# Expert lookup on one core: a quarter of the gathered down rows through TensorE, part of the coefficient products through ScalarE

## The chip, the cores and the metric

The kernel runs on one core of a Trainium2 chip. TensorE (PE) does matrix products, VectorE (DVE) and ScalarE (ACT) element-wise work and reductions, GpSimd (POOL) and SyncE (SP) issue transfers; 16 DMA engines of the core carry them. TensorE's clock has two levels, 2.4 and 1.2 GHz; the profile prints the granted one as 1.00 and 0.50. The metric is the time of one execution on the device, in microseconds (us), of the median run.

## What is computed

Two transformer blocks over 256 tokens of width 2048, in float32. Only the expert lookup of the first block ("PEER") is touched. Each token makes 8 queries (heads); each head picks 16 of 16,384 experts. An expert is one row of `expert_down` and one of `expert_up`; the token's activation is the dot product with the first, its output a weighted sum of the second:

```python
def peer(x, w_query, sub_keys, expert_down, expert_up):
    qry = (xt @ w_query).reshape(T, H, 2, PEER_HALF_DIM)
    s = jnp.einsum('thpd,phnd->thpn', qry, sub_keys).astype(jnp.float32)
    top_s, top_i = lax.top_k(s, K)
    ...
    best_s, best_pos = lax.top_k(cand_s.reshape(T, H, K * K), K)
    expert_idx = jnp.take_along_axis(cand_i.reshape(T, H, K * K), best_pos, axis=-1)
    gates = jax.nn.softmax(best_s, axis=-1).astype(x.dtype)
    ...
        u = expert_down[ib]
        act = jax.nn.gelu(jnp.einsum('td,thkd->thk', xb, u), approximate=False)
        vv = expert_up[ib]
        return jnp.einsum('thk,thkd->td', gb * act, vv)
```

## The kernel before

A tile is 128 tokens, one per partition; there are two, t = 0 and 1. With 8 heads each this makes 16 steps that are called heads 0 to 15 here. The lookup runs in these parts, all of them in one function.

**Queries.** `w_peer_query` is multiplied in four column blocks c (L681 on). SP loads the weights, ScalarE casts them to a high part (L253), VectorE makes the low part (L254, tile wlo), TensorE adds three products (L293 to L295, tile pq). ScalarE copies the result to qT (L685); TensorE and ScalarE make the scores of tile 0 block by block (`scores`, L677, L679), those of tile 1 when the first route of tile 1 is recorded. hn (L687) holds the normed tokens, one per partition.

**Routes.** `route(t, hd)` finds the 16 experts of a head on VectorE, 26 instructions or so from L569 to L606; L599 writes the expert indices (eidx) that the gathers need, L604 is an Exp on ScalarE.

**Down rows.** `peer_down(t, hd)`: for each of 16 experts k, POOL issues an indirect DMA that gathers one row of 2048 numbers per token (L612, 128 x 2048, 1.05 MB); two gathers share a row tile. VectorE multiplies the row with hn and sums along it (L621, CUSTOM_DVE_ANT_0 in the profile), one number per token, into dots. After 16 rows ScalarE applies Gelu (L625) and VectorE the gate (L626, output pk, since coef lies in that tile): this is a head's end.

**Coefficients of tile 0**, in the background of heads 8 to 11 (`store_coefs`, `coef_chunk`): for four tokens at a time ScalarE makes one-hot rows of the first index half (Square L648, Relu L649, tile ab), VectorE one-hot rows of the second half scaled by the coefficient (L667), TensorE multiplies them (L669, pcc), ScalarE copies the result to a chunk (L670). 32 such steps make 4 chunks of 2 MB; three go to DRAM (ct_d, ACT's queue), the last stays. Then `onehots_ahead` makes one-hot rows of tile 1 (tile oh) on ScalarE until the stage ends. Behind head 15 tile 1's products follow (L669 again), up to 1615 us, and then the "up" stage streams `expert_up`.

**What sets the order.** A scheduler places each instruction on its engine from the order of recording; `route_to` records routes some heads ahead, and the generator `bg` is advanced once for each pair of rows. Memory comes from pools: seven "big" tiles of 16 KB per partition (h, hn, hhi and hlo, qT, mhi and mlo earlier, row tiles, chunks), three raw tiles, two e8 tiles, and in PSUM two of 1024 columns (`acc`) and four of 512 (`pst`). A tile that is not free makes its writer wait, and POOL's gathers are issued in order, so a gather that waits holds up all later ones. Before the projection's end at 898 two row tiles are free, then five, while chunks are held three to five, then four.

```python
row = bigt([P, 2, D], name="row")
for i in range(2):
    gather(row[:, i, :], dn_d, eidx[:, t, hd, k + i:k + i + 1])
for i in range(2):
    V.tensor_tensor_reduce(out=row[:, i, :], in0=row[:, i, :], in1=hn[:, t, :], ...)
yield
```

## Time and profile before

| | us |
|---|---|
| median of 3 runs | 3214.01 (3211.68 to 3218.35) |
| the profiled execution | 3219.45, its span 3217.7 |
| the stage that is touched, from the first gather to head 15's end | 827 to 1574 |
| VectorE busy in the whole span | 2535.2 (79%) |
| TensorE busy in the whole span | 2555.4 (79%), mean granted clock 0.892 |
| DMA, mean over the span | 279 GB/s |

The page cuts the span into 40 slices. Slices 11 to 20 are the stage: VectorE and DMA stand at 9 tenths there, TensorE at 0 to 4 with its clock near 5 tenths. Elsewhere TensorE is at 9 and VectorE below. A view by stretch adds busy times of each engine between two moments; views by line group equal instructions; a timeline lists them in order of start, with the idle time before each and what ended it. An instruction's duration can overlap the next one's, so the distance of two starts is given as its pace.

### The profile page before, as it was taken

Reading aid. Unit: us, or ns where it says so; the run is one execution under the profiler, and the core shown is the slowest. Engines: PE = TensorE matmul, PEld = TensorE weight load, DVE = VectorE, ACT = ScalarE, POOL = GpSimd, SP = SyncE. Lnnn points to the kernel's source line nnn. Section 1 sums busy time; section 2 is a strip of 40 time slices with the busy share of each in tenths; the row PEclk is TensorE's granted clock in tenths of the full one; section 3 lists DMA queues with packets and bytes.
Section 4 is the critical chain, followed back from the end, with each engine's and each line's share of the span. In section 5 each row is a group of like instructions: output and inputs, shape, how many; then the busy total and the mean of one; then the engine's idle time right before and its main releaser. Section 6 shows DMA issues by size and latency. Waiting matters only on the chain. (4 is left out here: it accounts for less than half of the span.)

```text
span 3217.7 us, 35193 instructions
## 1 busy us (share of the span) xinstructions
PE 2555.4 (79%) x12368; PEld 2141.8 (67%) x12368; DVE 2535.2 (79%) x3682; ACT 1542.9 (48%) x2212; POOL 879.8 (27%) x575
## 2 busy tenths in 40 slices
PE   8999999999910004400399999999999999999999
PEld 7788888888810003300388888889987787878777
DVE  6656544555999999999988888887575799999974
ACT  5534444444310105441244444457445677778764
POOL 0000000000376686667766666620000000000000
PEclk9999999999965555555699999999999999999999
DMA  6455555565899999999789999974654599999964
GB/s 239 151 182 162 184 191 195 187 220 197 328 352 363 331 427 387 376 342 419 285 306 334 335 334 334 334 263 142 204 190 139 201 338 348 381 344 379 348 226 167
DMA packets 302522, 898.22 MB, mean 279 GB/s; under 512 B 20736, under 2 KB 42240, under 8 KB 268288
## 3 DMA queue, kind: packets, MB, share of 16 engines
q1 hardware_dynamic: 226560, 542.88, 48.1%
q0 software_dynamic: 57760, 335.65, 27.3%
q10 hardware_dynamic: 18016, 17.35, 1.6%
q8 instruction: 99, 1.62, 0.2%
q14 instruction: 87, 0.71, 0.1%
HBM read 887.42 MB, written 8.39 MB: 278 GB/s over the span
## 5 line engine op out<-in xcount | busy, mean ns | idle before, releaser
L254 DVE TENSOR_TENSOR wlo<-raw,whi 128x1024 fp32r<-128x1024 f32 (+1 forms) x538 | 648.5, 1208 | 453.1 <-ACT whi L253 446.9
L253 ACT CAST whi<-raw 128x1024 fp32r<-128x1024 f32 (+1 forms) x538 | 559.5, 1041 | 686.9 <-PE pj L284 255.6
L621 DVE CUSTOM_DVE_ANT_0 row<-row,hn 128x2048 f32<-128x2048 f32 x256 | 579.7, 2291 | 6.1 <-DMA row<-in_peer_expert_down_dram,eidx 5.7
L612 POOL DMA_INDIRECT row<-in_peer_expert_down_dram,eidx x256 | 508.4, 1986 | 265.8 <-DVE dots L621 100.7
L199 POOL TENSOR_TENSOR r<-rstdv,mhalf 128x2 f32<-128x2 f32 x5 | 4.5, 890 | 1508.9 <-DVE rstdv L225 1508.9
L612 POOL DMA_INDIRECT urow<-in_peer_expert_up_dram,eidx x256 | 322.8, 1261 | 197.7 <-DVE h L771 143.8
L254 DVE TENSOR_TENSOR wlo<-rawg,whi 128x1024 fp32r<-128x1024 f32 x256 | 313.1, 1225 | 35.1 <-ACT whi L253 10.3
L253 ACT CAST whi<-rawg 128x1024 fp32r<-128x1024 f32 x256 | 270.0, 1056 | 97.9 <-PE pgu L1283 68.6
L282 PE MATMUL pj<-whi,xhi 128*128 128x512 f32 x736 | 289.4, 393 | 1.3 <-ACT whi L253 1.3
L283 PE MATMUL pj<-wlo,xhi 128*128 128x512 f32 x736 | 288.6, 392 | 0.0
L284 PE MATMUL pj<-whi,xlo 128*128 128x512 f32 x736 | 288.2, 392 | 0.0
L639 PE MATMUL pcf<-cc,pk 128*128 128x128 f32 x2 | 0.9, 460 | 340.7 <-DVE pk L626 340.7
L639 PEld LDWEIGHTS pcf<-cc,pk 128*128 128x128 f32 x2 | 0.4, 182 | 341.5 <-issue 177.8
L1282 PE MATMUL pgu<-wlo,xs 128*128 128x512 f32 x512 | 199.8, 390 | 3.1 <-DVE wlo L254 3.1
L1281 PE MATMUL pgu<-whi,xs 128*128 128x512 f32 x512 | 200.0, 391 | 0.0
L1283 PE MATMUL pgu<-whi,xs 128*128 128x512 f32 x512 | 199.2, 389 | 0.0
L771 DVE SCALAR_TENSOR_TENSOR h<-urow,pk,h 128x512 f32<-128x512 f32 x256 | 191.8, 749 | 4.5
L254 DVE TENSOR_TENSOR wlo<-rawd,whi 128x1024 fp32r<-128x1024 f32 x128 | 154.1, 1224 | 12.1 <-ACT whi L253 1.1
L282 PEld LDWEIGHTS pj<-whi,xhi 128*128 128x128 f32 x736 | 138.5, 188 | 29.5 <-ACT whi L253 1.7
L284 PEld LDWEIGHTS pj<-whi,xlo 128*128 128x128 f32 x736 | 138.4, 188 | 28.1
L283 PEld LDWEIGHTS pj<-wlo,xhi 128*128 128x128 f32 x736 | 138.4, 188 | 27.7
L253 ACT CAST whl<-raw 128x1024 fp32r<-128x1024 f32 x96 | 101.2, 1056 | 113.5 <-PE ua L809 83.0
(547 smaller groups left out, 6302.0 us busy)
## 6 DMA issues: line engine op xcount, KB each, us to landing
raw<-in_w_in_dram SPq DMA_DIRECT2D x124, 1024.0 KB
raw<-in_peer_expert_up_dram SPq DMA_DIRECT2D x96, 1024.0 KB
rawg<-in_w_expert_gate_dram SPq DMA_DIRECT2D x128, 512.0 KB
rawg<-in_w_expert_up_dram SPq DMA_DIRECT2D x128, 512.0 KB
rawd<-in_w_expert_down_dram SPq DMA_DIRECT2D x64, 1024.0 KB
raw<-in_w_out_dram SPq DMA_DIRECT2D x32, 1024.0 KB
raw<-in_w_ret_branch_dram SPq DMA_DIRECT2D x16, 1024.0 KB
raw<-in_w_peer_query_dram SPq DMA_DIRECT2D x16, 1024.0 KB
```

Of the source, the lines that this page charges most:

```text
L199: G.tensor_tensor(out=dst, in0=v, in1=mhalf[:, 0:n], op=ALU.pow)
L253: S.copy(hi, raw)
L254: env["last"] = V.tensor_tensor(out=lo, in0=raw, in1=hi.bitcast(F32), op=ALU.subtract)
L282: TE.matmul(ps[:, t, :], h_, hi, start=st, stop=False)
L283: TE.matmul(ps[:, t, :], h_, lo, start=False, stop=False)
L284: env["mm"] = TE.matmul(ps[:, t, :], l_, hi, start=False, stop=en)
L612: G.indirect_dma_start(out=dst, out_offset=None, in_=src, in_offset=bass.IndirectOffsetOnAxis(ap=idx, axis=0))
L621: V.tensor_tensor_reduce(out=row[:, i, :], in0=row[:, i, :], in1=hn[:, t, :], scale=1.0, scalar=0.0, op0=ALU.mult, op1=ALU.add, accum_out= ...
L771: V.scalar_tensor_tensor(out=h[:, t, 1536:2048], in0=row[:, k, :], scalar=coef[:, t, c0 + k:c0 + k + 1], in1=h[:, t, 1536:2048], op0=ALU.m ...
L1281: TE.matmul(o_, xh, hi[:, :, i, :], start=k == 0, stop=False)
L1282: TE.matmul(o_, xh, lo[:, :, i, :], start=False, stop=False)
L1283: TE.matmul(o_, xl, hi[:, :, i, :], start=False, stop=k == NK - 1)
```

## The change

For k = 1, 5, 9 and 13 of heads 0 to 14 (60 of 256 rows) TensorE transposes the gathered row in 16 blocks (L619), ScalarE copies these from PSUM in two halves (L620, rT), TensorE multiplies them with the transposed hn (hT, new, both tiles; L653, pdd), and VectorE takes the diagonal of the 128 x 128 result (L631), two pairs of rows later; the Gelu and the gate (L636, L637) follow one pair late. Head 15 is done as before. hT takes one big tile, rT one e8 and one raw tile, and the scores of tile 1 move ahead of the first head, into a raw tile. For tile 0's coefficients, two of each four scaled one-hot rows are made on ScalarE (2 Squares, Relu, 2 multiplications by the coefficient, L683, L684, L705) in the place of VectorE (now L707). The chunks begin one pair of rows later, and `onehots_ahead` takes its tiles in another order and stops at 80 tokens until head 15.

```diff
+    def transposed_copy(dst, src):
+        for g in range(2):
+            ps = acc("pxT")
+            for j in range(8):
+                TE.transpose(ps[:, j // 4, j % 4 * P:(j % 4 + 1) * P], src[:, (g * 8 + j) * P:(g * 8 + j + 1) * P], ident)
+            S.copy(dst[:, g * 8:g * 8 + 8, :], ps.rearrange("p a (b c) -> p (a b) c", b=4))
+    def settle(n):
+        while late and late[0][0] <= n:
+            late.pop(0)[1]()
+    def diagonal(ps, dots, k):
+        junk = env["wk"].tile([P, P], F32, tag="dj", name="dj", bufs=1)
+        V.tensor_tensor_reduce(out=junk, in0=ps[:, 0:P], in1=ident, scale=1.0, scalar=0.0,
+                               op0=ALU.mult, op1=ALU.add, accum_out=dots[:, k:k + 1])
-    def peer_down(t, hd):
+    def peer_down(t, hd, on_pe, step):
...
+                if k + i in on_pe:
+                    rT = rTs[step[1] % 2]
+                    step[1] += 1
+                    transposed_copy(rT, row[:, i, :])
+                    ps = pst("pdd")
+                    for d in range(NK):
+                        TE.matmul(ps[:, 0:P], rT[:, d, :], hT[:, d, t * P:(t + 1) * P], start=d == 0, stop=d == NK - 1)
+                    late.append((step[0] + 2, lambda ps=ps, k=k + i: diagonal(ps, dots, k)))
...
+            settle(step[0])
+            step[0] += 1
             yield
+        late.append((step[0] + 1, lambda: peer_coefs(t, hd, dots)))
...
+            if not oh:
+                onehots(ab4[:, 1, 2:4], kT, c * 32 + q + 2, 2, 0)
             for i in range(4):
...
+                if not oh and i >= 2:
+                    S.mul(ab4[:, 1, i, :], ab4[:, 1, i, :], cT[:, tk:tk + 1])
...
+    sc_t[1] = raw_tile([P, 8, 2, P], "sc1")
+    for c in range(4):
+        scores(1, c)
+    hT = bigt([P, NK, T], name="hT")
+    for t in range(2):
+        transposed_copy(hT[:, :, t * P:(t + 1) * P], hn[:, t, :])
+    rTs = [e8([P, NK, P], name="rT"), raw_tile([P, NK, P], "rT")]
...
+            for j, _ in enumerate(peer_down(t, hd, () if pe_done else (1, 5, 9, 13), step)):
+                if n == 8 and j == 2:
+                    bg = store_coefs()
```

The order moves at three places. First, VectorE at the first row product of head 0 (row and dots): before, it stands amid the second route and the projection's splits (wlo).

```order
L254 TENSOR_TENSOR wlo_6046<-raw_6015,whi_6045 128x1024
L586 MAX bv_6617<-rtmp_6603 128x8
L602 TENSOR_SCALAR nm_6633<-bv_6617 128x1
L587 MAX_INDEX bp_6618<-bv_6617,rtmp_6603 128x8
L589 TENSOR_SCALAR ab_6624<-bp_6618 128x16
L590 TENSOR_SCALAR ab_6624<-bp_6618 128x16
L621 ISA row_6639,dots_6638<-row_6639,hn_5564 128x2048
L621 ISA dots_6638 128x1
L254 TENSOR_TENSOR wlo_6085<-raw_6082,whi_6084 128x1024
L254 TENSOR_TENSOR wlo_6113<-raw_6082,whi_6112 128x1024
```

Now it stands behind all splits and seven indices (L599), and routes stand between the row products that follow.

```order
L598 TENSOR_REDUCE pk_5594<-rtmp_7827 128x2x16
L573 MAX_INDEX i16_8058<-v16_8057,rtmp_8059 128x8
L599 SCALAR_TENSOR_TENSOR eidx_5595<-pk_5594 128x16
L578 TENSOR_TENSOR rtmp_8059<-v16_8057 128x256
L656 ISA row_6707,dots_6706<-row_6707,hn_5564 128x2048
L656 ISA dots_6706 128x1
L575 CAST if16_8070<-i16_8058 128x32
L583 MAX bv_8073<-rtmp_8059 128x8
L569 MAX v16_8094<-sc1_6563 128x8
```

In these two pieces 18 splits and nine routes have moved ahead of head 0's last row product, from behind it or from among its rows.

Second, TensorE from the projection's last scores (psr) to the first heads. Before, the products of the coefficients (pky, pcf, pcc) follow the scores at once, so that TensorE has nothing from head 0 to head 7 but the two pky transposes.

```order
L677 MATMUL psr_7131<-skT_5566,qT_5593 128x128 x4
L677 MATMUL psr_7137<-skT_5566,qT_5593 128x128 x4
L632 MATMUL pky_7346<-cc_84,pk_5594 128x128 x2
L639 MATMUL pcf_7351<-cc_84,pk_5594 128x128
L669 MATMUL pcc_7356<-ab4_7357 128x128 x4
```

Now hn's transposes stand there and then, row by row, the transposes (pxT) of a gathered row and its products (pdd).

```order
L717 MATMUL psr_6582<-skT_5566,qT_5593 128x128 x4
L619 MATMUL pxT_6589<-cc_84,hn_5564 128x128 x2
L619 MATMUL pxT_6599<-cc_84,hn_5564 128x128 x8
L619 MATMUL pxT_6609<-cc_84,hn_5564 128x128 x8
L619 MATMUL pxT_6619<-cc_84,hn_5564 128x128 x8
L619 MATMUL pxT_6711<-cc_84,row_6707 128x128 x8
L619 MATMUL pxT_6721<-cc_84,row_6707 128x128 x8
L653 MATMUL pdd_6731<-hT_6588,rT_6629 128x128 x16
L619 MATMUL pxT_6757<-cc_84,row_6753 128x128 x8
L619 MATMUL pxT_6767<-cc_84,row_6753 128x128 x8
L653 MATMUL pdd_6777<-hT_6588,rT_6630 128x128 x16
```

The transposes of one row stand behind the products of the row before it, without anything between them.

Third, ScalarE among the chunks, a step of four tokens. Before, a step is four Squares, a Relu (128x512) and a copy to the chunk.

```order
L648 ACTIVATE ab4_7462<-cc_84,kT_7349 128x128 x3
L670 COPY cchunk_7355<-pcc_7440 128x128x4
L648 ACTIVATE ab4_7462<-cc_84,kT_7349 128x128
L648 ACTIVATE ab4_7483<-cc_84,kT_7349 128x128
L649 ACTIVATE ab4_7462<-ab4_7462 128x512
```

Now the row copies (L620), the Gelu (L636) and the new multiplications (L705) stand in the same queue.

```order
L684 ACTIVATE ab4_9022<-ab4_9022 128x512
L636 ACT_TABLE_LOAD
L636 ACTIVATE pk_5594<-dots_8595 128x16
L620 COPY rT_6629<-pxT_8956 128x1024
L620 COPY rT_6629<-pxT_8966 128x1024
L683 ACTIVATE ab4_9022<-cc_84,kT_8692 128x128
L683 ACTIVATE ab4_9086<-cc_84,kT_8692 128x128
L684 ACTIVATE ab4_9022<-ab4_9022 128x256
L683 ACTIVATE ab4_9086<-cc_84,kT_8692 128x128
L705 ACTIVATE ab4_9022<-ab4_9022,cT_8696 128x128 x2
```

Between a step's Relu and its multiplications there stand copies that wait for TensorE's transposes of a gathered row, and a Gelu that waits for VectorE's dots.

## Rows read from the trace of the kernel before

**Rows 1.** Busy us by stretch: PE, PEld, DVE, ACT, POOL; clock, DMA share, GB/s

```profile
827.00:898.00 71.00, 60.91 (x452) 57.66 (x450) 63.17 (x88) 23.12 (x28) 28.31 (x20) 0.95 0.94 367
898.00:1212.00 314.00, 5.83 (x43) 5.01 (x43) 313.12 (x557) 26.52 (x60) 230.54 (x116) 0.52 0.96 375
1212.00:1424.00 212.00, 68.07 (x258) 55.55 (x258) 209.96 (x433) 90.79 (x223) 139.15 (x66) 0.53 0.95 364
1424.00:1574.00 150.00, 0.00 (x0) 0.00 (x0) 141.58 (x130) 38.68 (x117) 110.42 (x56) 0.50 0.98 407
```

**Rows 2.** Groups by line, 813 to 1574: count | busy us, mean ns | idle before

```profile
L621 DVE CUSTOM_DVE_ANT_0 row<-row,hn 128x2048 f32<-128x2048 f32 x256 | 579.7, 2291 | 6.1 <-DMA row<-in_peer_expert_down_dram,eidx 5.7
...
L667 DVE TENSOR_SCALAR ab<-cc,kT,cT 128x128 f32<-128x128 f32 x128 | 38.6, 372 | 0.0
...
L254 DVE TENSOR_TENSOR wlo<-raw,whi 128x1024 fp32r<-128x1024 f32 x22 | 26.8, 1222 | 4.3 <-ACT whi L253 2.7 <-issue 1.6
...
L604 ACT ACT_TABLE_LOAD x9 | 11.5, 1283 | 24.7 <-DVE nm L602 12.9 <-DVE bv L586 11.7
```

**Rows 3.** Timeline of VectorE near the stage's end: start, duration, [idle before]

```profile
1507.15 2.29 DVE L621 CUSTOM_DVE_ANT_0 row<-row,hn 128x2048 f32<-128x2048 f32 x1
...
1509.37 2.29 DVE L621 CUSTOM_DVE_ANT_0 row<-row,hn 128x2048 f32<-128x2048 f32 x1
...
1525.19 2.29 DVE L621 CUSTOM_DVE_ANT_0 row<-row,hn 128x2048 f32<-128x2048 f32 x1 [0.25 <-DMA row<-in_peer_expert_down_dram,eidx]
...
1530.08 2.29 DVE L621 CUSTOM_DVE_ANT_0 row<-row,hn 128x2048 f32<-128x2048 f32 x1 [0.26 <-DMA row<-in_peer_expert_down_dram,eidx]
```

**Rows 4.** Timeline of VectorE: ends of heads 0, 7, 11 and 15

```profile
897.96 0.17 DVE L626 TENSOR_TENSOR pk<-pk 128x16 f32<-128x16 f32 x1
...
1210.50 0.18 DVE L626 TENSOR_TENSOR pk<-pk 128x16 f32<-128x16 f32 x1 [0.28 <-ACT pk L625]
...
1423.77 0.18 DVE L626 TENSOR_TENSOR pk<-pk 128x16 f32<-128x16 f32 x1 [1.90 <-ACT pk L625]
...
1574.23 0.17 DVE L626 TENSOR_TENSOR pk<-pk 128x16 f32<-128x16 f32 x1
```

**Rows 5.** Two lines with their count and ns min/median/max, first and last start

```profile
L411 DVE CUSTOM_DVE_ANT_0 Pt<-psc,cc,sinks x16: 345/414/485, 87.9 to 118.1; 128x128 f32<-128x128 f32 x8, 128x256 f32<-128x256 f32 x8
...
L685 ACT COPY qT<-pq x8: 578/588/592, 808.5 to 898.2; 128x512 f32<-128x512 f32 x8
```

**Rows 6.** Timeline of TensorE: transposes at half clock, products at half, at full

```profile
3112.40 2.86 PE L311 MATMUL ptr<-cc,h 128*128 128x128 f32 x12 [5.30 <-PEq L1383]
...
1216.54 5.70 PE L669 MATMUL pcc<-ab 128*128 128x128 f32 x25 [1.26 <-DVE ab L667]
...
1575.79 27.59 PE L669 MATMUL pcc<-ab,oh 128*128 128x128 f32 x224 [0.85 <-DVE ab L667]
```

**Rows 7.** Timeline of VectorE's and ScalarE's coefficient work

```profile
1216.14 6.24 DVE L667 TENSOR_SCALAR ab<-cc,kT,cT 128x128 f32<-128x128 f32 x24
...
1425.04 1.26 ACT L648 ACTIVATE oh<-cc,kT 128x128 f32<-128x128 f32 x4
```

**Rows 8.** Groups by line on VectorE, 898 to 1212: the routes' indices

```profile
L599 DVE SCALAR_TENSOR_TENSOR eidx<-pk 128x16 int32<-128x16 f32 x9 | 1.6, 175 | 0.0
```

**Rows 9.** Timeline of POOL and VectorE: the first gather and the first row product

```profile
827.11 1.12 POOL L612 DMA_INDIRECT row<-in_peer_expert_down_dram,eidx  x1 [41.24 <-DVE eidx L599]
...
832.89 2.29 DVE L621 CUSTOM_DVE_ANT_0 row<-row,hn 128x2048 f32<-128x2048 f32 x1 [1.01 <-DMA row<-in_peer_expert_down_dram,eidx]
```

**Rows 10.** Busy us by short stretches, columns as in rows 1: TensorE's granted clock

```profile
1219.00:1222.00 3.00, 3.00 (x16) 3.00 (x15) 3.00 (x13) 2.29 (x5) 0.68 (x1) 0.50 1.00 423
1222.00:1225.00 3.00, 1.33 (x11) 1.14 (x9) 3.00 (x7) 2.52 (x8) 0.00 (x0) 0.95 1.01 426
1308.00:1314.00 6.00, 4.83 (x20) 4.41 (x20) 6.00 (x12) 3.96 (x8) 3.00 (x3) 0.50 0.93 348
3116.00:3120.00 4.00, 3.56 (x13) 2.67 (x14) 3.28 (x7) 3.40 (x8) 0.00 (x0) 0.50 0.00 0
```

More of the change, by code (lines that the diff above doesn't have):

```diff
@@ L612, in gather, with peer_coefs @@
         G.indirect_dma_start(out=dst, out_offset=None, in_=src, in_offset=bass.IndirectOffsetOnAxis(ap=idx, axis=0))
-    def peer_down(t, hd):
-        dots = sm.tile([P, 16], F32, tag="dots", name="dots")
+    def transposed_copy(dst, src):
[4 more added lines that the diff above has]
+            S.copy(dst[:, g * 8:g * 8 + 8, :], ps.rearrange("p a (b c) -> p (a b) c", b=4))
+    late = []
+    def settle(n):
[5 more added lines that the diff above has]
+                               op0=ALU.mult, op1=ALU.add, accum_out=dots[:, k:k + 1])
+    def peer_coefs(t, hd, dots):
+        c_ = coef[:, t, hd * 16:(hd + 1) * 16]
+        S.activation(c_, dots, AF.Gelu)
+        V.tensor_tensor(out=c_, in0=c_, in1=gates[:, t, hd, :], op=ALU.mult)
+    def peer_down(t, hd, on_pe, step):
+        dots = sm.tile([P, 16], F32, tag="dots", name="dots", bufs=3)
         for k in range(0, 16, 2):
@@ L620, in peer_down @@
             for i in range(2):
-                V.tensor_tensor_reduce(out=row[:, i, :], in0=row[:, i, :], in1=hn[:, t, :], scale=1.0, scalar=0.0,
-                                       op0=ALU.mult, op1=ALU.add, accum_out=dots[:, k + i:k + i + 1])
+                if k + i in on_pe:
[6 more added lines that the diff above has]
+                    late.append((step[0] + 2, lambda ps=ps, k=k + i: diagonal(ps, dots, k)))
+                else:
+                    V.tensor_tensor_reduce(out=row[:, i, :], in0=row[:, i, :], in1=hn[:, t, :], scale=1.0, scalar=0.0,
+                                           op0=ALU.mult, op1=ALU.add, accum_out=dots[:, k + i:k + i + 1])
+            settle(step[0])
+            step[0] += 1
             yield
-        c_ = coef[:, t, hd * 16:(hd + 1) * 16]
-        S.activation(c_, dots, AF.Gelu)
-        V.tensor_tensor(out=c_, in0=c_, in1=gates[:, t, hd, :], op=ALU.mult)
+        late.append((step[0] + 1, lambda: peer_coefs(t, hd, dots)))
     def key_rows(t):
@@ L691, in build @@
         scores(0, c)
-    order = [(t, hd) for t in range(2) for hd in range(8)]
+    sc_t[1] = raw_tile([P, 8, 2, P], "sc1")
[5 more added lines that the diff above has]
+    rTs = [e8([P, NK, P], name="rT"), raw_tile([P, NK, P], "rT")]
     routed = [0]
@@ L697, in route_to @@
             t, hd = divmod(routed[0], 8)
-            if (t, hd) == (1, 0):
-                sc_t[1] = e8([P, 8, 2, P], name="sc1")
-                for c in range(4):
-                    scores(1, c)
             route(t, hd)
@@ L718, in onehots_ahead @@
     def onehots_ahead(kT, oh1):
-        for n, mk in ((16, lambda: raw_tile([P, 16, P], "oh1")), (16, lambda: raw_tile([P, 16, P], "oh1")),
-                      (16, lambda: raw_tile([P, 16, P], "oh1")), (8, lambda: ws0.tile([P, 8, P], F32, tag="hi", name="oh1")),
+        for n, mk in ((8, lambda: ws0.tile([P, 8, P], F32, tag="hi", name="oh1")),
                       (8, lambda: ws0.tile([P, 8, P], F32, tag="lo", name="oh1")),
@@ L724, in onehots_ahead @@
                       (8, lambda: ws0.tile([P, 8, P], F32, tag="lo", name="oh1")),
-                      (16, lambda: e8([P, 16, P], name="oh1")), (16, lambda: e8([P, 16, P], name="oh1"))):
+                      (16, lambda: raw_tile([P, 16, P], "oh1")), (16, lambda: raw_tile([P, 16, P], "oh1")),
+                      (16, lambda: e8([P, 16, P], name="oh1")),
+                      (16, lambda: raw_tile([P, 16, P], "oh1")), (16, lambda: e8([P, 16, P], name="oh1"))):
+            while len(oh1) >= 20 and not pe_done:
+                yield
             tk = 4 * len(oh1)
@@ L731, in onehots_ahead @@
                 yield
-    kT1, oh1 = None, []
+    kT1, oh1, pe_done = None, [], []
+    step = [0, 0]
+    bg = iter(())
     for t in range(2):
-        bg = store_coefs() if t else iter(())
         for hd in range(8):
@@ L738, in build @@
             route_to(n + 2 + n // 6)
-            for _ in peer_down(t, hd):
-                if next(bg, 1) and t and kT1 is None:
+            if n == 15:
+                pe_done.append(1)
+            for j, _ in enumerate(peer_down(t, hd, () if pe_done else (1, 5, 9, 13), step)):
+                if n == 8 and j == 2:
+                    bg = store_coefs()
+                if next(bg, 1) and t and n > 8 and kT1 is None:
                     assert routed[0] == 16
```

10 lines of the change are left out of this document (6 added, 4 removed).

## The prediction

> **What bounds the kernel now.** I read the view of busy time by stretch first. Every change lies in the expert lookup's "down" stage, 813 to 1615 us. From the first gather to the end of head 15 VectorE is busy 63.17 of 71, 313.12 of 314, 209.96 of 212 and 141.58 of 150 us: it bounds the stage [rows 1]. The groups of instructions say with what: 256 row products of 2291 ns (L621), 128 coefficient products (L667), weight splits (L254) [rows 2], and the routes. Back to back one row product starts 2.21 us after the one before (1507.15 to 1509.37) [rows 3]. But the DMA column is not far behind: 0.94 to 0.98 of its capacity [rows 1], and at the end of the stage VectorE waits at every second row for a landing (1525.19, 1530.08): 4.89 us for two gathers, 2.45 us each [rows 3]. A gather is 128 x 2048 x 4 bytes = 1.049 MB, so this is 428 GB/s. **So the stage has two limits close together:** VectorE with 728 us of work between 827 and 1574 (the sum of the four stretches), and DMA with 256 x 2.45 = 627 us and 6.3 MB of stored chunks (14.7 us at 428 GB/s). Outside the stage the order on all engines is as before, so the forecast is the shift of its end, 1574.23 [rows 4].
>
> **Row products moved to TensorE.** 60 of 256 rows lose a VectorE product (2.21 us) and get a diagonal over 128 x 128 from PSUM. The nearest row is L411, the same kind of instruction from PSUM: 345 to 485 ns [rows 5]; I take 0.35, the 128-wide end. VectorE saves 60 x (2.21 - 0.35) = 112 us. TensorE gets 16 transposes and 16 products a row. Transposes: twelve in 2.86 us at the half clock, 0.23 each without the last one's tail, so 16 cost 3.7 us, and half of that, 1.8, at the full clock. Products: one is two records; 224 records in 27.59 us make 0.246 us each at the full clock, 25 in 5.70 us make 0.44 at the half clock, again without the tail [rows 6]; 16 cost 3.9 or 7.1. **One row on TensorE is 5.7 us at 2.4 GHz and 10.8 us at 1.2 GHz; four gathers bring one such row every 9.8 us.** ScalarE copies two 128 x 1024 blocks from PSUM; the nearest row is the 512-wide copy L685 at 588 ns [rows 5], so between 0.6 and 1.2 us each; I take 1.05, near twice its elements less one start: 2.1 us a row, covered in heads 1 to 7, where ScalarE is busy 26.52 us of 314 [rows 1].
>
> **Coefficient products on ScalarE.** 64 of 128 leave VectorE. One has a mean of 372 ns [rows 2], but they overlap; 24 took 6.24 us, 0.26 each: 17 us saved. On ScalarE four Squares take 1.26 us [rows 7]; with Relu and copy (0.5 each at this pace) a step of four tokens is 2.2 us, and 2 Squares, a half Relu and 2 multiplications make it 3.6. With one row's copies at every second pair that is 4.7 us a pair of gathers. Over the 32 steps of heads 8 to 11, with some 13 us of table loads and Gelus (1283 ns a load [rows 2]), it is 163 us. Here DMA needs 64 x 2.45 + 14.7 = 171.5, VectorE 48 x 2.21 + 16 x 0.35 + 64 x 0.26 + 5 routes of 7.3 = 165. (A route: from 898 to 1212 VectorE is busy 313 us [rows 1]; 112 rows at 2.21 leave 65 for nine routes [rows 8].) Three engines within 9 us of each other, and TensorE with 16 x (5.7 + 2.0) = 123 us at the full clock, 16 x (10.8 + 3.5) = 229 at the half.
>
> **What is lost at the start.** hT holds a big tile from the query projection on, so in the place of two row tiles before 898 and five behind it there are one and four. The gathers of pairs 1 to 3 wait for tiles that the projection's last matmuls and copies free: 2 gathers instead of 20 before the projection ends. TensorE has 60.91 us of work between 827 and 898 [rows 1]; without row products among its splits I put that end at 885. VectorE's order shows the second loss: the first row product stands behind seven routes, where two stood. Between the first index (just before 827 [rows 9]) and the end of head 0 VectorE now has 18 splits at 1.22 us (L254 [rows 2]), 9 more routes at 7.3, 13 rows at 2.21 and 4 diagonals: 22 + 66 + 29 + 2 = 119 us, 946 at the earliest; before, head 0 ended at 897.96 [rows 4]. From 885 with four tiles, and 5.8 us from release to landing (827.11 to 832.89 [rows 9]), the rows of head 0 wait among routes; I add 15 us: **960, with 26 gathers landed.** The 24 behind the first two are 59 us of DMA, so about 14 of the 75 us stand idle. This loss costs only DMA time: the routes would have come later anyway, among heads 1 to 7, which are now without them.
>
> **The sum.** Heads 1 to 7: 128 - 26 = 102 gathers at 2.45 = 250, and 5.8 for the last landing: 1216, against 1210.50 [rows 4]. VectorE's work there (84 rows, 28 diagonals: 196 us) is hidden. Heads 8 to 11: between 171.5 (DMA alone) and 213 (the time before, 1210.50 to 1423.77). Row tiles are three and for moments two while the chunks are held, so a late ScalarE or TensorE stops the gathers soon; I take the middle, 192: 1408. Heads 12 to 15: 157 us of DMA, less what is ahead, against 150 before; 155: **1563. That is 11 us earlier than 1574.** The tail to 1615 does the same products; I leave it. The profiled execution took 3219.45 us, so 3208 by it; its time is 5 us above the median 3214.01, and from the median it is 3203.
>
> A rule speaks against the whole gain. The Trainium skill, "DMA: Bandwidth & Descriptors", section "Bandwidth", holds that transfers from HBM to SBUF are bound near 358 GB/s per core. By that a gather would take 2.93 us, 256 of them 750 us, and the stage could not become shorter than it is: 3214. The trace disagrees: a gather every 2.45 us [rows 3]. I give it 0.01, inside the chance of no change.
>
> **Rivals.**
> *DMA alone sets the pace, no stalls (chance 0.12).* 885 + 254 x 2.45 + 14 us idle among the routes + 14.7 + 5.8 = 1541: 33 us earlier, 3181. For it: 0.98 of DMA already in the last stretch [rows 1]. Against it: three row tiles in heads 8 to 11.
> *Coupling eats the gain (0.24).* ScalarE's queue holds row copies, one-hot steps and the Gelu in one order; if each pair there costs its 5.36 us of DMA (171.5/32) and 1 us of waiting, heads 8 to 11 take 32 x 6.4 = 205 and the end is 1576: 3216, no change. For it: in this stretch VectorE was the one full engine (209.96 of 212 us, ScalarE 90.79 [rows 1]); now four are near full, and each waits for the others. Against it: each row has two pairs of slack before its diagonal is due.
> *TensorE stays at 1.2 GHz and becomes the bound (0.26): slower.* Its price decides once a row costs more than 9.8 us. Heads 8 to 11: 16 x (10.8 + 3.5) = 229; heads 12 to 14: 12 x 10.8 = 130; head 15, which has no such rows, 39: end at 1216 + 398 = 1614, 40 us later, 3254. If heads 1 to 7 go so too, 28 more us: 3282. For it: in the product stretches of before, TensorE busy 4.83 of 6 us (1308 to 1314) stayed at a granted clock of 0.50, the level of 1.2 GHz, and so did mostly transposes at 3.56 of 4 us (3116 to 3120). Against it: six us of unbroken products at 1216 to 1222 brought it to 0.95, and a TensorE that is the bound is never idle, with 7 us of products in each row [rows 10]. I hold that the clock rises within the products, so that a row comes out near the 9.8 us of its gathers; that this is so close is why the rival has this chance.
> The Trainium skill, "TensorE: Matmul & The Clock Gate", Part 4, says that transposes do not count as busy for the clock, and its section "HAM oscillation" that bursts with DMA waits between them start slowly each time. By both the time would be this rival's, 3254; the row of 3116 agrees with the first, and no run so far shows the second with bursts as long as these.
> *The naive sum (0.02, counted with the forecast's side).* If gathers could follow, VectorE's 112 + 17 us would leave: 3085. 2.45 us a gather stands against it.
>
> **How the numbers follow.** The forecast's case, heads 8 to 11 between 180 and 198 us, has 0.36; with the DMA floor and the naive sum 0.50 for faster. No change (within 0.2%, 6.4 us, about what a measurement of this kernel can tell) has 0.24, slower 0.26. The range goes from the DMA floor, 3181, to the rival of the half clock in heads 8 to 14, 3254; outside it lie the naive sum and a half clock in the whole stage, some 0.15. Likeliest: 3203; its own range is 3190 to 3209.
>
> **What would show it.** In the profile after: head 0 ends near 960, head 7 near 1216, with DMA at 0.98 or more and VectorE with a fifth of idle time that ends on landings. The granted clock over heads 1 to 7 should vary between 0.5 and 1; a plain 0.50 with TensorE over 95% busy is the slow rival, and then VectorE waits for the diagonal's PSUM tile and gathers for TensorE. Heads 8 to 11 near 192 us with ScalarE over 85% busy is my middle; 205 or more is the coupling. If head 7 ends much before 1216, the price of a gather was wrong; if head 0 ends much after 960, the start's loss was.

## The result and the profile after

The changed kernel takes 3266.66 us (median of 4 runs, 3259.62 to 3270.08) against 3215.29 for the kernel before, measured beside it: a ratio of 1.0157, with a 95% interval of 1.0136 to 1.0179. It is 51 us slower where 11 us faster was forecast, and it lies above the forecast's range (3181 to 3254).

The profiled execution took 3270.08 us. These are the ends of heads 0, 7, 11 and 15 in VectorE's timeline, which answer to [rows 4]:

```profile
957.43 0.17 DVE L637 TENSOR_TENSOR pk<-pk 128x16 f32<-128x16 f32 x1
...
1227.06 0.17 DVE L637 TENSOR_TENSOR pk<-pk 128x16 f32<-128x16 f32 x1 [0.28 <-ACT pk L636]
...
1466.95 0.17 DVE L637 TENSOR_TENSOR pk<-pk 128x16 f32<-128x16 f32 x1
...
1622.25 0.17 DVE L637 TENSOR_TENSOR pk<-pk 128x16 f32<-128x16 f32 x1
```

Set against the forecast, stretch by stretch (us):

| | before | forecast | after |
|---|---|---|---|
| end of head 0 | 898 | 960 | 957 |
| heads 1 to 7 | 312.5 | 256 | 269.6 |
| heads 8 to 11 | 213.3 | 192 | 239.9 |
| heads 12 to 15 | 150.5 | 155 | 155.3 |
| end of head 15 | 1574 | 1563 | 1622 |

Three of four terms came out within 14 us. Heads 8 to 11 missed by 48 us, most of the 59 by which the stage's end (1622 against 1563) missed. By stretch (columns as in [rows 1]) the profile after shows two quite different regimes:

```profile
885.00:925.00 40.00, 28.04 (x208) 26.50 (x208) 37.61 (x144) 13.47 (x23) 12.91 (x12) 0.89 0.75 287
925.00:957.00 32.00, 19.64 (x123) 18.54 (x123) 32.00 (x94) 8.05 (x12) 12.68 (x10) 0.76 0.78 302
...
957.00:1227.00 270.00, 189.65 (x1322) 182.63 (x1320) 199.15 (x234) 55.30 (x61) 201.65 (x111) 0.84 1.01 422
1227.00:1467.00 240.00, 154.20 (x1061) 148.83 (x1062) 170.41 (x373) 164.43 (x406) 85.82 (x66) 0.78 0.82 330
1467.00:1622.00 155.00, 78.52 (x546) 74.90 (x545) 114.07 (x129) 70.87 (x168) 98.00 (x56) 0.77 0.94 380
```

In heads 1 to 7 DMA is full (1.01, 422 GB/s) and VectorE has a quarter of its time free: the bound has moved to DMA, as forecast. In heads 8 to 11 nothing is full: TensorE is busy 154 of 240 us, VectorE 170, ScalarE 164, DMA 0.82. The loads are close to those of the forecast (VectorE 165, ScalarE 163), but each engine stands for 70 to 86 us. The view of waits, heads 8 to 11 (engine, tile and line, what it waited for: us in total, times, longest), shows for what:

```profile
DVE dj L631 <- PE pdd L653: 38.6, 10, 12.3
DVE row L656 <- DMA row<-in_peer_expert_down_dram,eidx: 19.7, 12, 3.1
...
PE pxT L619 <- DMA row<-in_peer_expert_down_dram,eidx: 41.2, 8, 10.6
PE pdd L653 <- ACT rT L620: 40.1, 13, 9.9
...
ACT cchunk L710 <- PE pcc L709: 48.7, 16, 6.6
ACT rT L620 <- PE pxT L619: 15.5, 9, 9.2
...
POOL row L612 <- DVE dots L656: 88.7, 11, 12.9
```

Read from the bottom: the gathers wait for VectorE to finish with row tiles, VectorE waits for a diagonal's products on TensorE, TensorE waits for ScalarE's row copies and for gathers, ScalarE waits for TensorE's coefficient products. One turn of it, in the timelines of TensorE, ScalarE, VectorE and POOL from 1256 on (start, duration, [idle before]):

```profile
1256.22 3.62 PE L619 MATMUL pxT<-cc,row 128*128 128x128 f32 x16
1269.77 6.27 PE L653 MATMUL pdd<-hT,rT 128*128 128x128 f32 x32 [9.93 <-ACT rT L620]
1275.88 1.95 PE L709 MATMUL pcc<-ab 128*128 128x128 f32 x16
...
1268.13 0.69 ACT L705 ACTIVATE ab<-ab,cT 128x128 f32<-128x128 f32 x2
1268.73 1.90 ACT L620 COPY rT<-pxT 128x1024 f32<-128x1024 f32 x2
1276.97 0.59 ACT L710 COPY cchunk<-pcc 128x512 f32<-128x512 f32 x1 [6.34 <-PE pcc L709]
...
1276.08 0.29 DVE L631 CUSTOM_DVE_ANT_0 dj<-pdd,cc 128x128 f32<-128x128 f32 x1 [12.31 <-PE pdd L653]
...
1281.00 0.95 POOL L612 DMA_INDIRECT row<-in_peer_expert_down_dram,eidx  x1 [13.91 <-issue]
```

TensorE had transposed the row by 1259.8. ScalarE was in the middle of coefficient steps that stand ahead of the row copy in its queue, and copied only at 1268.73. TensorE stood 9.93 us for the copy; sixteen records of coefficient products stood behind the row's products and ran without a gap at 1275.88. VectorE stood 12.31 us for the diagonal, with row products behind it, and POOL issued no gather from 1267 to 1281.

### The profile page after: what moved, and what is told of

It is laid out like the page before. It is cut to its first block, busy times and chain, and to the rows that moved or that the text cites. A ratio compares the mean times of both kernels' runs of the same rounds, so it can differ in the third digit from the quotient of the medians.

```text
span 3268.3 us, 41509 instructions
## 1 busy us (share of the span) xinstructions
PE 2949.7 (90%) x15280; PEld 2521.0 (77%) x15280; DVE 2410.9 (74%) x3618; ACT 1696.0 (52%) x2488; POOL 782.9 (24%) x575
## 5 line engine op out<-in xcount | busy, mean ns | idle before, releaser
L656 DVE CUSTOM_DVE_ANT_0 row<-row,hn 128x2048 f32<-128x2048 f32 x196 | 446.3, 2288 | 96.4 <-DMA row<-in_peer_expert_down_dram,eidx 87.7
L612 POOL DMA_INDIRECT row<-in_peer_expert_down_dram,eidx x256 | 413.2, 1614 | 403.7 <-issue 126.5
L653 PE MATMUL pdd<-hT,rT 128*128 128x128 f32 x1920 | 276.9, 312 | 85.1 <-ACT rT L620 85.1
L653 PEld LDWEIGHTS pdd<-hT,rT 128*128 128x128 f32 x1920 | 269.1, 227 | 94.8 <-ACT rT L620 94.7
L253 ACT CAST whi<-rawg 128x1024 fp32r<-128x1024 f32 x256 | 269.3, 1053 | 101.7 <-PE pgu L1335 72.3
L619 PE MATMUL pxT<-cc,row 128*128 128x128 f32 x960 | 155.9, 332 | 138.0 <-DMA row<-in_peer_expert_down_dram,eidx 137.8
L620 ACT COPY rT<-pxT 128x1024 f32<-128x1024 f32 x120 | 118.5, 1010 | 259.3 <-PE pxT L619 258.9
L619 PEld LDWEIGHTS pxT<-cc,row 128*128 128x128 f32 x960 | 141.2, 174 | 144.9 <-issue 141.7
```

What stands on the lines that cost most here:

```text
L253: S.copy(hi, raw)
L612: G.indirect_dma_start(out=dst, out_offset=None, in_=src, in_offset=bass.IndirectOffsetOnAxis(ap=idx, axis=0))
L619: TE.transpose(ps[:, j // 4, j % 4 * P:(j % 4 + 1) * P], src[:, (g * 8 + j) * P:(g * 8 + j + 1) * P], ident)
L653: TE.matmul(ps[:, 0:P], rT[:, d, :], hT[:, d, t * P:(t + 1) * P], start=d == 0, stop=d == NK - 1)
```

## Experiments

Ends and lengths of the stretches, each from one profiled execution, with the median time of each kernel (us; ratio to the kernel before, measured beside it):

| run | head 0 ends | 1 to 7 | 8 to 11 | 12 to 15 | time | ratio (95%) |
|---|---|---|---|---|---|---|
| before | 898 | 312.5 | 213.3 | 150.5 | 3215 | |
| after | 957 | 269.6 | 239.9 | 155.3 | 3266.66 | 1.0136 to 1.0179 |
| e1 products back | 958 | 269.4 | 219.6 | 165.6 | 3254.29 | 1.0108 to 1.0143 |
| e2 no rows 8 to 11 | 958 | 270.2 | 201.3 | 162.9 | 3235.21 | 1.0047 to 1.0080 |
| e3 neither | 957 | 269.3 | 211.6 | 160.8 | 3243.64 | 1.0071 to 1.0104 |
| e4 products alone | 895 | 312.6 | 198.1 | 149.3 | 3195.99 | 0.9926 to 0.9959 |
| e5 late hT | 900 | 305.1 | 201.6 | 166.1 | 3216.37 | 1.0000 to 1.0020 |
| e6 rows in 1 to 7 | 900 | 305.4 | 202.6 | 149.0 | 3203.85 | 0.9955 to 0.9980 |
| e7 copies on VectorE | 958 | 269.6 | 240.9 | 158.1 | 3272.74 | 1.0166 to 1.0200 |
| e8 two steps ahead | 957 | 269.1 | 226.6 | 165.5 | 3260.80 | 1.0126 to 1.0160 |
| e9 diagonal 4 late | 958 | 269.2 | 238.8 | 160.7 | 3271.26 | 1.0163 to 1.0194 |
| e10 no chunk tiles | 966 | 268.2 | 235.4 | 155.9 | 3267.96 | 1.0158 to 1.0189 |
| e11 spread routes | 900 | 289.9 | 210.6 | 142.0 | 3190.40 | 0.9918 to 0.9945 |
| e12 spread, rows 1 to 11 | 903 | 289.1 | 247.0 | 131.9 | 3219.40 | 1.0005 to 1.0027 |
| e13 chunk copy cut | 966 | 268.5 | 235.5 | 156.3 | 3272.61 | one run |
| e14 row copy cut | 957 | 268.3 | 201.9 | 169.3 | 3240.50 | one run |
| e15 diagonal cut | 957 | 268.6 | 228.2 | 166.1 | 3259.78 | one run |
| e16 three products | 903 | 287.8 | 198.3 | 142.7 | 3173.60 | 0.9855 to 0.9888 |
| e17 products behind | 958 | 268.1 | 219.5 | 153.5 | 3243.96 | 1.0075 to 1.0106 |
| e18 rows 1 to 11 behind | 901 | 287.2 | 238.4 | 133.6 | 3205.74 | 0.9958 to 0.9982 |

**The parts undone, and one part alone.** e1 takes the coefficient products back to VectorE:

```diff
-            if not oh:
-                onehots(ab4[:, 1, 2:4], kT, c * 32 + q + 2, 2, 0)
...
-                if not oh and i >= 2:
-                    S.mul(ab4[:, 1, i, :], ab4[:, 1, i, :], cT[:, tk:tk + 1])
...
```

> The changed kernel, but all four of each four coefficient products are made on VectorE again; the rows on TensorE stay. Theory Q (queues): in heads 8 to 11 the row copies stand in ScalarE's queue behind coefficient steps, TensorE's products of the row wait for them, its coefficient products stand behind those, ScalarE's chunk copies wait for these, and VectorE's diagonals and through them the row tiles come late; 240 us instead of 213. A step is 1.4 us shorter on ScalarE here (2.2 instead of 3.6), so the row copies come earlier: heads 8 to 11 in 205 to 225 us, the whole at 3232 to 3252. Rival L (load): the longer steps alone make the loss, then heads 8 to 11 fall below 195 and the whole is near 3220. Rival T (tiles): the big tile that the transposed tokens hold leaves too few row tiles; then heads 8 to 11 stay at 230 to 245 and the whole at 3257 to 3270.

Heads 8 to 11 came to 219.6 us, as theory Q said; the whole, 3254, is 2 us over its range. e2 takes the rows out of heads 8 to 11 instead, and e3 does both:

```diff
-            for j, _ in enumerate(peer_down(t, hd, () if pe_done else (1, 5, 9, 13), step)):
+            for j, _ in enumerate(peer_down(t, hd, () if pe_done or 8 <= n < 12 else (1, 5, 9, 13), step)):
```

> The changed kernel, but in heads 8 to 11 all rows are multiplied on VectorE; heads 0 to 7 and 12 to 14 keep their rows on TensorE, and half of the coefficient products stay on ScalarE. Theory Q: without row copies and diagonals the ring of waits is gone; VectorE has 64 x 2.21 + 64 x 0.26 + 5 x 7.3 = 195 us, so heads 8 to 11 take 195 to 205, and the whole comes out at 3218 to 3232: the same as before, since the start still costs 17 us up to head 7 and the last heads 5. Rival L: ScalarE's long steps still hold, heads 8 to 11 above 220. Rival T: above 225, the whole above 3250.

> As the run without rows in heads 8 to 11, and all coefficient products on VectorE too: heads 8 to 11 do what they did before the change, with one big tile less for rows. Theory Q: VectorE is the bound again with 212 us, as before; 213 to 220, the whole at 3235 to 3245. Rival T: the missing tile shows here alone: 230 or more, 3250 or more.

201.3 and 211.6 us, the second a little under its range. Without rows VectorE is the bound again: in e2's view by stretch it is busy 195.60 of 202 us.

```profile
1228.00:1430.00 202.00, 64.74 (x243) 53.78 (x243) 195.60 (x371) 131.22 (x373) 132.74 (x64) 0.54 0.96 365
```

e3 does in heads 8 to 11 what the kernel before does, with hT's tile missing, in the same time (211.6 and 213.3): a row tile less costs nothing there. e2's whole, 3235, is a little over its range, since heads 12 to 15 took 163 us. e4 is the kernel before with e1's removed lines added.

> The kernel before, with only the second part of the change: two of each four coefficient products of tile 0 on ScalarE; no rows on TensorE, no transposed tokens. Theory Q: VectorE is the bound in heads 8 to 11 and loses 64 x 0.26 = 17 us; heads 12 to 15 then start with fewer gathers ahead and run at the DMA's 2.45 us, so 5 to 10 of the 17 come back: the whole 7 to 14 us faster, 3201 to 3208. Rival L: ScalarE's longer steps (3.6 instead of 2.2 us, 115 us in all) delay TensorE and the chunks: no gain, 3212 to 3225.

It gained 16 us, 2 more than expected; heads 12 to 15 gave nothing back. So the products on ScalarE save 15 us where no rows go to TensorE (213.3 to 198.1), save 10 in e2 against e3, and cost 20 where rows do (219.6 to 239.9). Rows cost 8 us beside the old products (211.6 to 219.6) and 39 beside the new (201.3 to 239.9). **Neither part loses much alone; together they do.**

**The start.** e5 transposes hn behind head 0 (and leaves head 0 and heads 8 to 11 without rows), e6 leaves heads 12 to 15 without rows as well:

```diff
-    hT = bigt([P, NK, T], name="hT")
...
+            if n == 1:
+                hTs.append(bigt([P, NK, T], name="hT"))
+                for u in range(2):
+                    transposed_copy(hTs[0][:, :, u * P:(u + 1) * P], hn[:, u, :])
```

> The changed kernel with two differences: hn is transposed behind head 0 instead of ahead of it, so hT takes its big tile later, and rows go to TensorE only in heads 1 to 7 and 12 to 14 (4 of 16 as before). Against the run without rows in heads 8 to 11 only the start differs. If the loss at the start (head 0's end 957 instead of 898) is hT's tile and the order that follows from it, head 0 ends near 898 here, heads 1 to 7 take the 270 us that DMA needs (1168), heads 8 to 11 the 201 of VectorE's load, the last four 160: end 1530, the whole 3165 to 3180. Rival: the gathers that start earlier are not gained, since routes have to come anyway; then head 7 ends at 1205 or later and the whole is 3205 or more.

> As the run with late transposed tokens, but heads 12 to 15 are all on VectorE, so rows go to TensorE in heads 1 to 7 alone and hT's tile is free from head 8 on. The last heads are bound by DMA (2.45 us a gather), so the rows there gain nothing and their copies stand behind the one-hot rows on ScalarE: heads 12 to 15 in 157 instead of 163 us, and the whole 3 to 10 us below the other, near 3165. If they do gain, it is above it.

Head 0 ended at 900, so the 58 us at the start come from hT's early place, as the prediction had it, together with head 0's rows on TensorE, which need hT and went with it. But heads 1 to 7 then took 305 us, not 270, and both runs missed what was expected (3165 to 3180, and near 3165). e5 came out as its rival said: of the 58 us only 24 were left at head 7's end (1205 against 1228 in e2), and 19 in the whole. Heads 12 to 15 took 149 us in e6 against 166 in e5, so rows on TensorE, with hT's tile that they hold, lose there too. Heads 1 and 2 took 59 and 53 us. By stretch, e6 has VectorE full there and DMA at 0.82:

```profile
950.00:1012.00 62.00, 36.64 (x245) 35.26 (x244) 61.98 (x187) 14.12 (x22) 24.26 (x18) 0.79 0.82 310
```

Rows moved to TensorE had only let routes of later heads move forward on VectorE: by the count of L599, four and three fall in heads 1 and 2, where the kernel before has two in each. e11 holds a route until the last VectorE row of the head before is done, by a copy of one column into a tile that the route writes first:

```diff
+        if after is not None:
+            V.tensor_copy(v16[:, 0, 0:1], after[:, 15:16])
...
```

> As the run with rows on TensorE in heads 1 to 7 alone and late transposed tokens, and each route of head 2 and later is held until the last VectorE row of the head just recorded is done (a copy of one column on VectorE makes it wait): about one route per head. There heads 1 and 2 took 58 and 54 us with VectorE full of routes and DMA idle for 16 of 100 us, heads 3 to 7 ran at DMA's 38.5 us. If that front load is what kept the gain away, heads 1 to 7 now take 270 to 280 us (84 rows at 2.21, 28 diagonals at 0.29, 8 routes at 7.3 = 252 us of VectorE, 274 of DMA) instead of 305, and the whole is 3170 to 3185. If DMA's rate falls when routes stand among rows, they stay at 295 or more, the whole above 3195.

Heads 1 to 7 took 290 us, 10 above their range, with DMA at 1.01 in the same stretch, and the whole 3190, 5 us above its range. The routes were a part of it; 16 us over DMA's 274 remain. Heads 8 to 11, to which a part of the VectorE work moved, took 8 us more than in e6, and the last heads 7 less.

**Which wait holds heads 8 to 11.** The first theory (Q) put it on ScalarE's queue. e8 lets ScalarE be two steps ahead of TensorE at most, e7 moves the row copies to VectorE:

```diff
-            ab4 = w4([P, 2, 4, P], name="ab4")
...
+                ab4 = abs_[q // 4 % 2]
```

```diff
-                    transposed_copy(rT, row[:, i, :])
+                    transposed_copy(rT, row[:, i, :], V.tensor_copy if t and hd < 4 else None)
```

> The changed kernel, but the coefficient steps of tile 0 use two fixed one-hot tiles in turn instead of four from the pool, so ScalarE can be two steps ahead of TensorE at most; same work. Theory Q says the row copies then stand behind two steps (about 7 us) at most, not four or five (16 us): heads 8 to 11 in 215 to 232 us, the whole 3240 to 3258. If the run-ahead does not matter, they stay at 240 and the whole at 3266; if TensorE's products starve for one-hot rows, it is slower than that.

> The changed kernel, but in heads 8 to 11 VectorE copies the transposed rows from PSUM (32 copies of 128 x 1024), not ScalarE; all else stays. VectorE's sum in these heads goes from 165 to about 202 us (about 1.15 us a copy, an estimate from its 1.22 us for the weight split of the same size). Theory Q: the row copies no longer stand behind coefficient steps: heads 8 to 11 in 205 to 222 us, the whole 3233 to 3252, although VectorE has more to do. Rival: it is the number of row tiles or TensorE that holds these heads; then the copies' 37 us come on top or change nothing: 240 us or more, the whole 3262 or more.

e8 was in its range for heads 8 to 11 (226.6); heads 12 to 15 gave most of it back, and the whole, 3261, is 3 us over. e7 was not: 240.9. **ScalarE's queue alone is not the cause.** The waits of e7 show why: VectorE has a queue too, and TensorE stood for the copies as before.

```profile
PE pdd L653 <- DVE rT L620: 48.3, 17, 5.8
...
ACT cchunk L710 <- PE pcc L709: 75.9, 19, 7.3
```

e9 gives diagonals four pairs instead of two (the Gelu and the start of the chunks come two pairs later as well), e10 gives heads 8 to 10 a fourth row tile:

```diff
-                    late.append((step[0] + 2, lambda ps=ps, k=k + i: diagonal(ps, dots, k)))
+                    late.append((step[0] + 4, lambda ps=ps, k=k + i: diagonal(ps, dots, k)))
...
```

```diff
-        cc_ = bigt([P, P, 32], name="cchunk")
+        scr = None if oh or c == 3 else scratch()
+        cc_ = bigt([P, P, 32], name="cchunk") if scr is None else None
...
```

> The changed kernel, but VectorE takes each diagonal four pairs of rows late instead of two (and the Gelu follows three pairs late instead of one); same work. Moving the row copies to VectorE left heads 8 to 11 at 241 us, so ScalarE's queue alone is not the cause. Theory R (ring): gathers wait for VectorE's rows, these stand behind a diagonal, this waits for TensorE's products, these for a row copy, this for the transposes and the work ahead of it, and the transposes for the gathers; four queues in order, closed in a ring with room for two pairs. With room for four pairs VectorE no longer stands (38.6 us of waiting for diagonals in these heads), and heads 8 to 11 fall to 195 to 218, the whole to 3225 to 3245. Rival W (room for rows): it is three and at times two row tiles that let no lead build up, whoever waits; then it stays at 230 to 240, the whole at 3255 to 3267.

> The changed kernel, but the first three chunks of tile 0 are copied to a small scratch tile and normed tokens are stored in their place (so the output is not the reference's): same instructions on ScalarE and the same bytes stored, but row tiles are four until head 10. Theory R: two gathers more of lead shorten the waits a little: heads 8 to 11 in 222 to 235 us. Rival W: with four tiles, as in heads 1 to 7, the lead is back: heads 8 to 11 in 185 to 210, the whole 3215 to 3240.

Both theories fell: 238.8 and 235.4 us. Neither room for VectorE nor room for gathers brought the four heads down by more than 5 us. One head did change: with a fourth row tile head 8 took 53 us instead of 69, but heads 9 to 11 then took 183 instead of 171. What had stayed in each was TensorE's wait for row copies, here in e9 (heads 8 to 11):

```profile
PE pdd L653 <- ACT rT L620: 56.5, 14, 8.5
```

e12 combines e11, rows in heads 1 to 11 and e9's late diagonals.

> As the run with spread routes, with rows on TensorE in heads 8 to 11 too, and diagonals four pairs late. Theory R: heads 8 to 11 then come near the three engines' loads (163 to 171 us) plus some waiting, 180 to 200, and the whole is 3150 to 3175. Rival W: row tiles hold them at 220 or more, and the whole is 10 us or more above the run with spread routes alone.

247 us, worse than in the changed kernel (six routes fall in these heads here, five there). Rival W had such a number, but e10 speaks against W. Then each link was cut by itself. e13 (on top of e10) copies one-hot rows to the scratch tile, e14 multiplies a fixed block, e15 takes the diagonal of the identity:

```diff
+                S.copy(scr[:, :, q % 16:q % 16 + 4], ab4[:, 0].rearrange("p t i -> p i t"))
```

```diff
-                        TE.matmul(ps[:, 0:P], rT[:, d, :], hT[:, d, t * P:(t + 1) * P], start=d == 0, stop=d == NK - 1)
+                        TE.matmul(ps[:, 0:P], hT[:, d, 0:P] if t and hd < 4 else rT[:, d, :], hT[:, d, t * P:(t + 1) * P], start=d == 0, stop=d == NK - 1)
```

```diff
-                    late.append((step[0] + 2, lambda ps=ps, k=k + i: diagonal(ps, dots, k)))
+                    late.append((step[0] + 2, lambda ps=ident if t and hd < 4 else ps, k=k + i: diagonal(ps, dots, k)))
```

> The run without chunk tiles, but for the first three chunks ScalarE copies one-hot rows of the same size to the scratch tile instead of TensorE's products, which nobody reads (output not the reference's): ScalarE keeps its work but no longer waits for coefficient products. Theory P (pair): TensorE and ScalarE wait for each other in turn, ScalarE's chunk copy for products that stand behind a row's products, TensorE's row products for copies that stand behind the chunk copy. With this link cut, heads 8 to 10 take 45 to 50 us each instead of 56 (1234 to 1404 without the cut), heads 8 to 11 190 to 212. If the pair is not it, 228 to 240.

> The changed kernel, but in heads 8 to 11 TensorE multiplies a fixed block of the transposed tokens instead of the copied row (output not the reference's); the row copies are still made on ScalarE, nobody waits for them. Theory P: this cuts the same ring at its other link: heads 8 to 11 in 190 to 212 us. If instead VectorE's or the gathers' waits are the cause, 228 to 240.

> The changed kernel, but in heads 8 to 11 the diagonal is taken of the identity in SBUF instead of TensorE's result (output not the reference's): VectorE no longer waits for TensorE's row products. Theory P: VectorE's wait was only the end of the chain; TensorE and ScalarE still wait for each other, and the coefficient products on VectorE and the transposes follow them: heads 8 to 11 in 215 to 240 us. Theory R (the ring through VectorE and the gathers): 190 to 212.

Only e14 brought heads 8 to 11 down, to 201.9 us. e15 stayed at 228.2: VectorE's wait was mostly the end of the chain. e13 stayed at 235.5, against its expectation: ScalarE's wait for the chunk copy came back as a wait for the one-hot tiles (ACT ab waiting for PE pcc, 23.2 us), so that cut did not open the link, and it says little on the pair. e14 has a flaw too: the scheduler, freed of the wait, also placed the products otherwise, among the coefficient products. e17 therefore leaves nothing out and places a row's products behind the next row's transposes in TensorE's queue. Diagonals, Gelu and the start of the chunks are as late as in e9, so e9 is the run to set it against:

```diff
+                    last = transposed_copy(rT, row[:, i, :])
+                    flush(last)
+                    pend_row.append((rT, t, dots, k + i))
...
+                with tc.issue_after(last.ins):
+                    products(*pend_row.pop(0))
```

> The changed kernel, nothing left out, but in heads 8 to 11 TensorE multiplies a row only behind the transposes of the next row (diagonals follow two pairs after that), so that a row copy has the time of two pairs, some 10 us, before TensorE stands for it. Theory P (TensorE, which works in order, stands for the row copy and holds up the coefficient products and the transposes behind it): heads 8 to 11 in 195 to 218 us instead of 240, the whole 3228 to 3248. If the wait was not the link, 230 to 242 and 3257 to 3270.

219.5 us and 3244 for the whole, 23 us better than the changed kernel (heads 8 to 11 1.5 us over the range, the whole inside it). Against e9 heads 8 to 11 are 19 us shorter. In its waits, heads 8 to 11, the products' wait is gone and the transposes wait for gathers:

```profile
PE pxT L619 <- DMA row<-in_peer_expert_down_dram,eidx: 55.4, 11, 10.5
PE pxT L619 <- ACT ab L701: 9.6, 2, 6.5
...
PE pdd L641 <- ACT rT L620: 2.8, 1, 2.8
```

The views by stretch of e9 and then of e17 show a second difference:

```profile
1227.00:1466.00 239.00, 148.46 (x1011) 142.60 (x1011) 167.76 (x369) 159.11 (x391) 85.81 (x65) 0.79 0.82 321
...
1226.00:1446.00 220.00, 142.28 (x1048) 138.23 (x1049) 173.21 (x379) 164.60 (x405) 119.22 (x68) 0.84 0.91 358
```

The products now follow transposes at once, and TensorE's granted clock is 0.84 instead of 0.79. How much of the 19 us is the wait and how much the clock, no run separates.

Heads 9 to 11 now take 50 us each, as in e14 (after: 57). Head 8, where the coefficient work starts, still takes 69 us as in the changed kernel; e14 has 52 there. POOL stands there twice for some 11 us until VectorE is done (1254 to 1265, 1272 to 1283); whether e10's fourth row tile would help here, no run tried.

**A version that beats both.** e16 is e11 with three of four coefficient products on ScalarE:

```diff
-                onehots(ab4[:, 1, 2:4], kT, c * 32 + q + 2, 2, 0)
+                onehots(ab4[:, 1, 1:4], kT, c * 32 + q + 1, 3, 0)
...
```

> The run with spread routes (rows on TensorE in heads 1 to 7 alone), and three of each four coefficient products of tile 0 on ScalarE instead of two. VectorE is the bound in heads 8 to 11 there (210 us) and loses 32 x 0.26 = 8 us, ScalarE's step grows from 3.6 to 4.3 us, 139 us in all, below VectorE's: the whole 3 to 8 us faster, 3182 to 3188; no change if the last heads give it back at DMA's pace.

It takes 3173.60 us, below its range (3182 to 3188), 1.3% below the kernel before and 17 us below e11, more than the 8 us of VectorE's work: heads 8 to 11 fell by 12 and end there at 1389, VectorE busy 197.89 of 199 us. e18 adds rows in heads 8 to 11, with e17's order.

> The run with three coefficient products on ScalarE, late transposed tokens and spread routes, with rows on TensorE in heads 8 to 11 too, multiplied one row later as above. Theory P: VectorE, the bound there with 198 us, loses 16 x 1.9 = 30 us and heads 8 to 11 come to 180 to 195, of which the last heads give a part back at DMA's pace: the whole 3160 to 3172 against 3174. If ScalarE's steps (4.3 us) with row copies (1 us a pair) and Gelus, some 185 us, still close a ring, heads 8 to 11 take 205 or more and the whole 3180 or more.

It missed: 238.4 us and 3206, as its second case said. With 184 us of ScalarE work in these heads, rows on TensorE cost more than VectorE saves, in this order as well. TensorE's wait for row copies is not among its waits there (it stands 32.3 us for gathers, 20.0 for VectorE's one-hot rows and 28.7 for ScalarE's), and POOL waits 22.3 us for indices of routes. So this loss has another link, and which one is open.

## Why the prediction was wrong

**The bound and its move: right.** VectorE's loads came out as summed (diagonals 289 ns, expected 350; 170 us of work in heads 8 to 11, expected 165), and DMA took over in heads 1 to 7 at 422 GB/s. The naive sum's rival fell as argued. The Trainium skill's limit of some 358 GB/s ("DMA: Bandwidth & Descriptors", section "Bandwidth"), which the same section gives for two cores that share an HBM domain and both stream, is not seen with this one core: the trace has 422 over 270 us, and the measurement decides.

**The start: right in mechanism and place** (960 against 957; e5, without the early hT, ends head 0 at 900). The idle time of DMA that the prediction puts at 14 of 75 us is 16 by its own terms (75 less 59), which moves nothing but the first rival, by 2 us. Of its size one part was off: 26 gathers were to have landed by then. 287 GB/s over 40 us and 302 over 32 are 21.1 MB, 20 gathers, and two before: 22. That is 10 of the 14 us by which heads 1 to 7 ran over 256.

**The failed step: heads 8 to 11, "I take the middle, 192".** The loads were right and the bounds were not. I took the time before, 213, as the upper end, as if a stretch whose fullest engine has less to do could not become slower. But the change put TensorE, ScalarE and VectorE, each working in order, behind one another in a ring: transposes, row copy, products, diagonal, row tile, gather. The upper end should have come from one turn of that ring. Worked out from the prediction's prices, as an estimate made after the result: two coefficient steps of 3.6 us and a row's copies of 2.1 on ScalarE, then 1.8 of transposes, 3.9 of row products and 2.0 of coefficient products on TensorE at the full clock, one behind the other, are 17 us for a row, 272 us for 16. The measured 240 are 15 a row, between that and the 10.7 of full overlap.

**The rivals.** The coupling rival named this mechanism (ScalarE's queue with row copies, one-hot steps and Gelu in one order) and sized it at 1 us a pair, 205 us; it was 2.1 us a pair. Its "two pairs of slack before its diagonal is due" was no protection, since TensorE stood long before VectorE did. The slow rival came near the size (end at 1614, measured 1622) by luck: TensorE was not the bound. Its clock was 0.84 in heads 1 to 7 and 0.78 in heads 8 to 11, and it was busy only 154 of 240 us there. Still the clock has a part in the ring, since the full clock would make 123 us of the 154 by the prediction's sum.

**What is shown and what is open.** Shown: rows and products on ScalarE lose much only together (e1 to e4); taking TensorE's wait for row copies away, with all work kept, brings back about half of the loss in heads 8 to 11 (e17 against e9, with the clock that follows), and the wait is there whichever engine copies (e7); room for diagonals or for rows alone does not help (e9, e10). e14, which cuts the link, brings back nearly all of it, in one run and with another order of the products. Not settled: the share of the clock, why rows lose in e18, and why head 8 keeps its 69 us in e17 (54 in e2). That last is most of the 18 us by which e17's heads 8 to 11 still exceed e2's; the changed kernel exceeds them by 39.

**Heads 12 to 15: right in number, in part by luck** (155 and 155.3). The runs add that this stretch gives back a part of what heads 8 to 11 gain: it ranges from 132 us (e12) to 169 (e14), long where the stretch ahead was short. With heads 8 to 11 at 201 us, near the forecast's 192, e2 took 163.

## What to carry to other kernels

Work that is moved to an idle engine can close a ring if its result comes back through engines that work in order: bound such a stretch from above by one turn of the ring in series, not by the time before. Where an engine waits for a copy of its own earlier result, put the other work that is ready between the two in its queue (19 us in e17; in e18, with more work on ScalarE, it was not enough). And before relieving an engine, see what a scheduler will pull forward into the space: here it was routes of later heads, and holding them back was worth 13 us.

## What the runs showed of the hardware

TensorE at some 70% busy in heads 1 to 7, rows of transposes and products with gaps for gathers between, had a mean granted clock of 0.84 and took 189.65 us for 28 rows (6.8 us each, between the 5.7 and 10.8 worked out). Its timeline shows rows at both levels:

```profile
1010.89 3.65 PE L619 MATMUL pxT<-cc,row 128*128 128x128 f32 x16 [4.64 <-DMA row<-in_peer_expert_down_dram,eidx]
1014.33 4.29 PE L653 MATMUL pdd<-hT,rT 128*128 128x128 f32 x32
1020.64 1.94 PE L619 MATMUL pxT<-cc,row 128*128 128x128 f32 x16 [2.02 <-DMA row<-in_peer_expert_down_dram,eidx]
1022.86 3.84 PE L653 MATMUL pdd<-hT,rT 128*128 128x128 f32 x32 [0.28 <-ACT rT L620]
```

In heads 1 to 7 the 16 transposes took 3.40 to 3.65 us, the half clock, behind waits of 3.7 us and more, and 1.94 us, the full clock, behind waits of 2.0 us and less; behind waits of 2.5 to 3.0 us they took from 1.94 to 3.60. The Trainium skill's rule that bursts with waits between them start slowly each time ("TensorE: Matmul & The Clock Gate", section "HAM oscillation") is seen behind the longer of these waits, and not behind the short ones. Products right behind such slow transposes took 4.29 us, and 6.27 behind the wait of 9.93 in the turn at 1256: the transposes had helped to raise the clock, which is against the first of the two rules that the slow rival cites. In the kernel before, at 4.83 of 6 us busy, the clock stayed at 0.50 [rows 10].

A copy of 128 x 1024 from PSUM took 1010 ns on ScalarE and 1214 on VectorE, as these groups of the changed kernel (813 to 1622) and of e7 (heads 8 to 11) show:

```profile
L620 ACT COPY rT<-pxT 128x1024 f32<-128x1024 f32 x120 | 118.5, 1010 | 259.3 <-PE pxT L619 258.9
```

```profile
L620 DVE COPY rT<-pxT 128x1024 f32<-128x1024 f32 x32 | 38.5, 1214 | 0.2 <-PE pxT L619 0.2
```
